# Hybrid decoder layer on one core: four merge steps built among the last branch steps, and a new order for those steps

## The chip, the cores and the metric

The kernel runs on one core of one Trainium2 chip. The metric is the device time of one execution in microseconds, as the median over several runs; lower is better.

## The reference, cut to what matters

One post-norm decoder layer over x of shape (1, 256, 1024) in float32. One input projection feeds four causal token mixers (A: RG-LRU, B: gated DeltaNet, C: stick-breaking attention, D: GLA). Each mixer's output is projected back to 1024 columns, gated, and summed; then come an output projection, a LayerNorm, and a mixture of 16 experts with top-2 routing.

```python
proj = jnp.einsum("bsd,de->bse", x, w_in)
(a_in, gdn_qkv, gdn_beta_in, gdn_decay_in, gdn_gate_in,
 sb_qkv, gla_qkv, gla_lr, gla_gate_in, merge_in) = jnp.split(proj, offsets, axis=-1)
...
gates = jax.nn.sigmoid(merge_in.reshape(b, s, N_BRANCHES, D_MODEL))
merged = jnp.zeros_like(x)
for n, y_n in enumerate((y_a, y_b, y_c, y_d)):
    merged = merged + gates[:, :, n] * jnp.einsum("bsc,cd->bsd", y_n.astype(x.dtype), w_branch[n])
return jnp.einsum("bsd,de->bse", merged, w_out)
```

## The kernel before

The program is one function, `trunk`, which emits the instructions of five engines. It has three parts: the branch steps, sixteen merge steps with the output projection behind them, and the mixture of experts.

**Precision.** A float32 product is made of three products of a faster kind: each operand is split into a high part and a remainder. For weights this is `parts` (lines 117 to 134): ScalarE casts the raw tile to `whi` (L129), VectorE subtracts to get `wlo` (L133). There are three buffers of each (NHI = 3), so a cast waits until TensorE is done with the tile three casts before it. `mm3` (L268 to L280) issues the products: sixteen on `whi` and eight on `wlo` for one 1024 x 128 block. Raw weights of 1 MB come by DMA from SyncE's queue (`fetch`, L116) into three buffers; SyncE issues in the order of the program and waits at a buffer that is not free.

**Branch steps.** The string `ORDER` lists them, and a loop calls `steps[f]` in that order. Steps with `_in` in their function's name are projections (`bi`, `gg`, `lg`, `dq`, `dv`, `cq`, `cv`, `ai`): TensorE work that depends on nothing but the weights. The others are chains with many engines in turn. Those that matter here, by the names in `ORDER`:

- `b1` (`b_s1`, L620): the second chunk of DeltaNet. TensorE `pr`, VectorE scales and adds it into `VB` (L624), TensorE `pvn` (from `VB`) and `pos`, ScalarE copies `vn` (L628), TensorE `po` (from `vn`), VectorE adds `ob` (L634), ScalarE sums the squares (`junk`, L599).
- `cw`, `ct`, `cy` (L785 to L842): stick-breaking attention in three pieces: `cw` makes scores (`pze`, `pzo`), a tanh `sth` on ScalarE (L802), two GpSimd operations and a memset (L804, L807, L809), scans on VectorE (`ss`, L811), and weights in `sth` (L813). `ct` transposes them on TensorE (`pwt`, L826) and ScalarE copies them to `wt`; `cy` multiplies by the values (`pyc`).
- `gg.1` is the second half of DeltaNet's gate projection (`ptm`, then `th` on ScalarE and `gg` on VectorE, L657 and L658); `by` norms and gates DeltaNet's output (`fb`, `ytok` L642, transposes `pyt` L646, `yth` and `ytl`); `do` and `dy` are the same for GLA; `ai.0` and `ai.1` are the RG-LRU input projection (`pcm`) with its convolution on VectorE (`xc`, L852); `al` is the RG-LRU itself: products `prg` (L862), a row of activations `tr`, `ti`, `aa` (L863 to L867), VectorE and GpSimd operations with a scan (`ya`), and a split into `yth`, `ytl`.

**Merge steps.** `merge(i)` for i = 0 to 15: projects one 256-column block of a branch's gate (48 products `pcm`), takes a tanh on ScalarE (`tg`, L897), multiplies the branch's output by its block of `w_branch` (24 products `pbr`), and adds gate times product into `acc` on VectorE (L906 to L909). The branches come in the order `MORDER = (1, 3, 2, 0)`, so steps 0 to 3 belong to B (DeltaNet), 4 to 7 to D, 8 to 11 to C, and 12 to 15 to A. From step 6 on (RS = 6) each step also issues some expert weights ahead (L946).

**What sets the order.** SyncE's queue is kept in program order. On the other four engines a scheduler decides, when the kernel is built, which ready instruction comes next, and it prefers steps that are written earlier; on the chip each engine then runs its own list in that fixed order and waits at semaphores. So the order in which steps are written decides which work stands beside a chain that waits. PSUM has eight banks: three for the projections (`mm`) and five for the rest (`pb`).

Of the kernel before, what the change touches and what calls it, by code (L numbers as in the profile page):

```python
# [29 lines left out]
NPJ = 8  # L30
NH2 = 15
RS = 6
RAW0 = 1
NHI = 3
NRA = 20
# [4 lines left out]
ORDER = """  # L40
bi.0 cc bi.1 bi.2 cq.0 bi.3 sm bi.4 cq.1 bi.5 bs gg.0 bp.0 ll bv.0 cq.2 bp.1 bo lg.0
dq.0 ba.1 lg.1 bb dq.1 dq.2 dq.3 bx.0 ba.0 dv.0 bx.1 dg bl.0.0 dv.1 bl.1.0 bl.0.1 cq.3 de
bl.2.0 da.0 bl.1.1 da.1 bv.1 cw.0 cv.0 b0 bl.2.1 rt ds cw.2 do.1 b1 ct.0 do.0 cw.1 cv.1 ct.2 cy.0
gg.1 ct.1 ai.0 cy.1 by ai.1 dy al
"""

C_A, C_GQ, C_GBD, C_GG, C_SQ, C_SV = 0, 512, 2048, 2056, 2568, 3592
# [4 lines left out]
def trunk(ctx: ExitStack, tc: tile.TileContext, a, out):  # L52
# [11 lines left out]
    rwp = [r.enter_context(tc.tile_pool(name="rw", bufs=1, side="left")) for r in rws]  # L64
    rwo = [(0, 2, 1)[(RAW0 + j) % 3] for j in range(3)]

    def turn_raw():
        rwo.append(rwo.pop(0))
# [23 lines left out]
    def Y(name, dt=F32R):  # L92
        return yp.tile([128, 4, S], dt, name=name, tag="y", bufs=NY)

    def pb(name, shape=(128, 4, 128)):
        return pbr.tile(list(shape), F32, name=name, tag="pb")
# [12 lines left out]
    def fetch(src, cuts=1):  # L109
        k, n = src.shape[1], src.shape[2]  # L110
        turn_raw()
        raw = rwp[rwo[-1]].tile([128, 2048], F32, name="raw", tag="raw")[:, :k * n]
        raw = raw.rearrange("p (k c) -> p k c", k=k)
        for c in range(cuts):
            cs = slice(c * n // cuts, (c + 1) * n // cuts)
            Q.dma_start(raw[:, :, cs], src[:, :, cs])  # L116
        return raw

    def parts(raw, k0, nk, c0, n, one=None):

        hi = wst.tile([128, 1024], F32R, name="whi", tag="whi", bufs=NHI)[:, :nk * n]
        lo = wst.tile([128, 1024], F32R, name="wlo", tag="wlo", bufs=NHI)[:, :nk * n]
        hi = hi.rearrange("p (k c) -> p k c", k=nk)
        lo = lo.rearrange("p (k c) -> p k c", k=nk)
        src = raw[:, k0:k0 + nk, c0:c0 + n]
        cuts = (slice(0, nk),) if one is None else (slice(0, nk // 2), slice(nk // 2, nk))
        for c in cuts:
            if one is None:
                A.copy(hi, src)  # L129
            else:  # L130
                A.activation(hi[:, c], src[:, c], AF.Copy, scale=one)  # L131
        for c in cuts:
            V.tensor_tensor(lo[:, c], src[:, c], hi[:, c].bitcast(F32), op=OP.subtract)  # L133
        return hi, lo
# [104 lines left out]
    for lv in range(3):  # L239
        s = 16 << lv  # L240
        m = pmask[:, lv, :]
        if s < 64:
            m = m.rearrange("p (b r) -> p b r", r=s)
# [24 lines left out]
    def mm3(o, sh, sl, mh, ml, kt, first=True, last=True, wm=False):  # L268

        for k in range(kt):  # L270
            T.matmul(o, sh(k), mh(k), start=first and k == 0, stop=False)  # L271
            if wm:
                T.matmul(o, sl(k), mh(k), start=False, stop=False)  # L273
            else:
                T.matmul(o, sh(k), ml(k), start=False, stop=False)  # L275
        for k in range(kt):
            if wm:
                T.matmul(o, sh(k), ml(k), start=False, stop=last and k == kt - 1)
            else:
                T.matmul(o, sl(k), mh(k), start=False, stop=last and k == kt - 1)  # L280

    def proj_cm(c0, raw=None, one=None):

        if raw is None:
            raw = fetch(w_in[:, :, c0:c0 + 256])
        p = pmm.tile([128, 2, S], F32, name="pcm", tag="mm")
        for b in range(2):
            hi, lo = parts(raw, 0, 8, 128 * b, 128, one)
            mm3(p[:, b, :], lambda k: hi[:, k, :], lambda k: lo[:, k, :],
                lambda k: xh[:, k, :], lambda k: xl[:, k, :], 8)  # L290
        return p
# [357 lines left out]
    def gate_in(nm, c0, ci):  # L649

        if ci == 0:
            setattr(v, nm, PJ(nm, (128, 2, 512)))
        g = getattr(v, nm)
        p = proj_tm(c0 + 256 * ci)
        for t in range(2):
            th = tmp.tile([128, 256], F32, name="th", tag="thp")
            A.activation(th, p[t], AF.Tanh, scale=0.5)  # L657
            V.scalar_tensor_tensor(g[:, t, 256 * ci:256 * ci + 256], th, 1.0, p[t], op0=OP.add, op1=OP.mult)  # L658
# [226 lines left out]
    def merge(i):  # L885

        bi, c4, c2 = i // 4, i // 2 % 2, i % 2
        b = MORDER[bi]
        if i == 0:
            v.acc = [Y("acc0", F32), Y("acc1", F32)]  # L890
        if c2 == 0:
            v.rawb = fetch(wbr[b].rearrange("(k p) c -> p k c", p=128)[:, :, c4 * 512:(c4 + 1) * 512])
        p = proj_cm(C_M + b * D + (4 * c4 + 2 * c2) * 128)
        if c2:
            turn_raw()
        tg = wst.tile([128, 2, S], F32, name="tg", tag="tg", bufs=2)
        A.activation(tg, p, AF.Tanh, scale=0.5)  # L897
        p = pb("pbr", (128, 2, S))
        hi, lo = parts(v.rawb, 0, 4, 256 * c2, 256)
        for j in range(2):  # L900
            cs = slice(j * 128, (j + 1) * 128)
            mm3(p[:, j, :], lambda k: hi[:, k, cs], lambda k: lo[:, k, cs],
                lambda k: yth[b][:, k, :], lambda k: ytl[b][:, k, :], 4)
        ac = v.acc[c4][:, 2 * c2:2 * c2 + 2, :]
        if bi == 0:
            V.scalar_tensor_tensor(ac, tg, 1.0, p, op0=OP.add, op1=OP.mult)  # L906
        else:
            V.scalar_tensor_tensor(tg, tg, 1.0, p, op0=OP.add, op1=OP.mult)
            V.tensor_tensor(ac, ac, tg, op=OP.add)  # L909
# [3 lines left out]
        bv=b_vb, b0=b_s0, b1=b_s1, by=b_y,  # L913
        gg=lambda c: gate_in("gg", C_GG, c), lg=lambda c: gate_in("lg", C_LG, c),
# [3 lines left out]
        cw=c_w, ct=c_t, cy=c_y, ai=a_in, al=a_lru, m=merge, cc=consts, ll=late_loads, rt=router_consts)  # L918
# [49 lines left out]
    def run_ahead(n):  # L968
        for _ in range(n):
            key, src = ahead.pop(0)  # L970
            W[key] = load(src, rings, NRA + NRX + NY + 4)

    for i in range(16):
        merge(i)
        if i >= RS:
            run_ahead((i + 1 - RS) * NRA // (16 - RS) - (i - RS) * NRA // (16 - RS))
        if i == 11:
            for n in range(2):
                Q.dma_start(x_sb[n], xin[:, n, :])
# [473 lines left out]
```

## Time and profile before

| | |
|---|---|
| median of 3 runs | 617.74 us (616.12 to 619.96) |
| profiled execution, its own time | 617.43 us |
| its span in the trace | 615.6 us (1.8 us lie around it) |
| branch steps | from 0 to about 221 us of the span |
| merge steps 0 to 15 | from about 212 to 353 us |
| output projection and routing | 353 to 389 us |
| experts | 389 to 604 us |
| TensorE busy | 95% of the span |

All times of rows are microseconds from the start of the span. PE is TensorE, PEld its weight load, DVE VectorE, ACT ScalarE, POOL GpSimd, SPq SyncE's DMA queue. A float32 product shows as two records on PE; a product of split parts as one. Records of PE overlap, since products are pipelined and their ends are modelled: the distance between starts tells the rate.

### The profile page before, as it was taken

The page shows a single profiled execution, that of the slowest core. Times are in us where ns is not written, and L with a number is a line of the kernel's source. Part 1 is how long each engine was busy: PE and PEld are TensorE (multiplying, and loading weights), DVE is VectorE, ACT ScalarE, POOL GpSimd, SP SyncE. Part 2 cuts the span into 40 slices and gives each one's busy share as a digit, 9 for nine tenths or more (in the row PEclk, how much of TensorE's full clock was granted, in tenths as well). Part 3 has the DMA queues.
Part 4 walks back from the last instruction along what each step waited for, and adds up shares of the span by engine and source line. Part 5 has one row for each costly group of instructions (what it writes and reads, how often), then busy time and mean ns, then how long its engine had stood idle before and what let it go on. Part 6 is the DMA issues. An engine that isn't in the chain of part 4 may idle for free. (4 is left out here: it accounts for less than half of the span.)

```text
span 615.6 us, 10554 instructions
## 1 busy us (share of the span) xinstructions
PE 587.5 (95%) x4231; PEld 459.4 (75%) x4231; DVE 323.8 (53%) x651; ACT 253.4 (41%) x413; POOL 18.8 (3%) x53
## 2 busy tenths in 40 slices
PE   6999999999988999999999999999999999999992
PEld 5999999989978999999999999633533534444351
DVE  3798887677465986555565655542210300121245
ACT  5556664563469784443434544311211211021121
POOL 3000010100111000000000000000000000000000
PEclk9999999999999999999999999999999999999996
DMA  7877453742220436588998895889999999999941
GB/s 207 230 224 196 137 162 128 210 133 71 70 70 8 156 123 201 187 301 327 357 365 300 264 404 184 304 328 399 417 414 409 414 415 409 416 417 407 417 168 71
DMA packets 86380, 160.43 MB, mean 261 GB/s; under 512 B 9963, under 2 KB 56161, under 8 KB 86326
## 3 DMA queue, kind: packets, MB, share of 16 engines
q1 hardware_dynamic: 86198, 159.44, 71.5%
q8 instruction: 35, 0.57, 0.4%
q0 software_dynamic: 128, 0.26, 0.2%
q14 instruction: 19, 0.16, 0.1%
HBM read 158.50 MB, written 1.18 MB: 259 GB/s over the span
## 5 line engine op out<-in xcount | busy, mean ns | idle before, releaser
L133 DVE TENSOR_TENSOR wlo<-raw,whi 128x1024 fp32r<-128x1024 f32 (+1 forms) x106 | 125.9, 1200 | 53.3 <-ACT whi L129 52.6
L129 ACT CAST whi<-raw 128x1024 fp32r<-128x1024 f32 x102 | 105.9, 1048 | 101.4 <-PE pcm L275 34.8
L271 PE MATMUL pcm<-xh,whi 128*128 128x256 f32 x512 | 126.1, 284 | 2.3 <-ACT whi L131 1.5
L275 PE MATMUL pcm<-xl,whi 128*128 128x256 f32 x512 | 125.0, 282 | 0.0
L271 PEld LDWEIGHTS pcm<-xh,whi 128*128 128x128 f32 x512 | 97.4, 190 | 3.2 <-ACT whi L131 1.9
L275 PEld LDWEIGHTS pcm<-xl,whi 128*128 128x128 f32 x512 | 97.4, 190 | 0.1
L280 PE MATMUL pcm<-xh,wlo 128*128 128x256 f32 x512 | 72.5, 283 | 0.3 <-DVE wlo L133 0.2
L280 PEld LDWEIGHTS pcm<-xh,wlo 128*128 128x128 f32 x512 | 65.8, 190 | 0.8 <-DVE wlo L133 0.7
L101 DVE TENSOR_TENSOR dd<-pd,dd 128x512 fp32r<-128x512 f32 (+1 forms) x18 | 11.4, 632 | 95.3 <-ACT dd L100 95.3
L1301 PE MATMUL pd<-ew,sh 128*64 128x512 f32 (+1 forms) x288 | 56.8, 546 | 0.7 <-ACT sh L1362 0.7
L1290 PE MATMUL wu<-ew,xg 128*64 128x512 f32 x256 | 57.4, 593 | 0.0
L1290 PE MATMUL wg<-ew,xg 128*64 128x512 f32 x256 | 56.7, 595 | 0.6 <-issue 0.6
L1301 PEld LDWEIGHTS pd<-ew,sh 128*64 128x64 f32 x288 | 20.4, 137 | 35.1 <-issue 30.3
L1290 PEld LDWEIGHTS wu<-ew,xg 128*64 128x64 f32 x256 | 18.5, 137 | 36.2 <-issue 34.7
L1290 PEld LDWEIGHTS wg<-ew,xg 128*64 128x64 f32 x256 | 18.1, 137 | 33.5 <-issue 32.4
L271 PE MATMUL ptm<-whi,xh 128*128 128x256 f32 x128 | 32.6, 287 | 0.0
L271 PE MATMUL pbr<-yth,whi 128*128 128x256 f32 x128 | 32.1, 284 | 0.0
L275 PE MATMUL pbr<-ytl,whi 128*128 128x256 f32 x128 | 32.0, 282 | 0.0
L273 PE MATMUL ptm<-whi,xl 128*128 128x256 f32 x128 | 31.6, 281 | 0.0
L100 ACT CAST dd<-pd 128x512 fp32r<-128x512 f32 (+1 forms) x18 | 9.7, 539 | 46.3 <-PE pd L1301 46.3
L1207 ACT ACTIVATE xg<-pxg,gbp 128x128 f32<-128x128 f32 x32 | 13.3, 456 | 36.7 <-DVE xg L1206 35.8
L1341 DVE SCALAR_TENSOR_TENSOR sh<-wu,cw,sh 128x512 f32<-128x512 f32 x8 | 6.0, 751 | 37.9 <-PE wu L1290 37.8
(421 smaller groups left out, 887.5 us busy)
## 6 DMA issues: line engine op xcount, KB each, us to landing
raw<-in_w_in_dram SPq DMA_DIRECT2D x39, 1024.0 KB, 5.3
ew<-in_w_gate_dram SPq DMA_DIRECT2D x64, 512.0 KB, 9.8
ew<-in_w_up_dram SPq DMA_DIRECT2D x64, 512.0 KB, 9.6
ew<-in_w_down_dram SPq DMA_DIRECT2D x64, 512.0 KB, 9.8
raw<-in_w_branch_dram SPq DMA_DIRECT2D x8, 1024.0 KB
raw<-in_w_out_dram SPq DMA_DIRECT2D x4, 1024.0 KB
x<-in_x_dram SPq DMA_DIRECT2D x4, 256.0 KB, 5.3
raw<-in_w_in_dram SPq DMA_DIRECT2D x2, 512.0 KB
```

The costliest lines, as they stand in the source:

```text
L100: A.copy(hi, ps)
L101: V.tensor_tensor(lo, ps, hi.bitcast(F32), op=OP.subtract)
L129: A.copy(hi, src)
L133: V.tensor_tensor(lo[:, c], src[:, c], hi[:, c].bitcast(F32), op=OP.subtract)
L271: T.matmul(o, sh(k), mh(k), start=first and k == 0, stop=False)
L273: T.matmul(o, sl(k), mh(k), start=False, stop=False)
L275: T.matmul(o, sh(k), ml(k), start=False, stop=False)
L280: T.matmul(o, sl(k), mh(k), start=False, stop=last and k == kt - 1)
L1207: A.activation(xg[1][:, 2 * kg + k, :], ps[kg][:, k, 128:256], AF.Identity, scale=g_, bias=b_)
L1290: P(T.matmul(p[r, :], xg[pr][:, k, r], W[pr, (nm, e, k // 2)][:, k % 2, :], start=k == 0, stop=k == 7))
L1301: P(T.matmul(p[r, :], hT[:, k, r], W[pr, ("wd", e, k)][:, 0, c0:c1], start=k == 0, stop=k == 3))
L1341: V.scalar_tensor_tensor(sg, pu, cw[pr // 2][:, pr % 2:pr % 2 + 1], sg, op0=OP.mult, op1=OP.mult)
```

## The change

Four merge steps (m.0 to m.3, all of branch B) are taken out of the merge loop and written into `ORDER` among the last branch steps, and these get another order: `cw.2` comes behind `b1`; `cv.1`, `cw.1`, `gg.1`, `ai.0` and `by` come forward; `ct.2`, `cy.0`, `ct.1` and `cy.1` go behind them; `al` stands between m.2 and m.3. No instruction's computation is changed, and the number of products is the same.

```diff
@@ -30,6 +30,7 @@
 NPJ = 8
 NH2 = 15
 RS = 6
+MB = 4
 RAW0 = 1
@@ -40,8 +41,8 @@
-bl.2.0 da.0 bl.1.1 da.1 bv.1 cw.0 cv.0 b0 bl.2.1 rt ds cw.2 do.1 b1 ct.0 do.0 cw.1 cv.1 ct.2 cy.0
-gg.1 ct.1 ai.0 cy.1 by ai.1 dy al
+bl.2.0 da.0 bl.1.1 da.1 bv.1 cw.0 cv.0 b0 bl.2.1 rt ds do.1 b1 cw.2 ct.0 do.0 cv.1 cw.1 gg.1
+ai.0 by ct.2 ai.1 cy.0 dy m.0 ct.1 m.1 cy.1 m.2 al m.3
 """
@@ -971,7 +972,8 @@
     for i in range(16):
-        merge(i)
+        if i >= MB:
+            merge(i)
         if i >= RS:
```

Lines below the first hunk move by one, those below the last by two. Up to the product that makes GLA's state (`pst` of `ds`) all five engines' lists are the same as before, and SyncE's and GpSimd's lists are the same throughout.

First, TensorE around `b1`, before. `VB_1984` is the operand that VectorE makes for `pvn`; the `ptm` rows are products of `gg.1`.

```order
L278 MATMUL ptm<-wlo,xh 128x256 x3
L604 MATMUL pvn<-VB_1984,XT_1629 128x128
L604 MATMUL pos<-st,gq 128x128 x4
L278 MATMUL ptm<-wlo,xh 128x256
L271 MATMUL ptm<-whi,xh 128x256
L273 MATMUL ptm<-whi,xl 128x256
L604 MATMUL pvn<-VB_1984,XT_1629 128x128
L271 MATMUL ptm<-whi,xh 128x256
L604 MATMUL pvn<-VB_1984,XT_1629 128x128
```

The same place with the change: `pol` and its second half come from `do.1`.

```order
L607 MATMUL pol<-stl,qd 128x128
L605 MATMUL pvn<-VB_1984,XT_1629 128x128 x4
L605 MATMUL pos<-st,gq 128x128 x4
L605 MATMUL po<-vn,AN_1264 128x128 x4
L800 MATMUL pze<-sk,sq 128x256
L800 MATMUL pzo<-sk,sq 128x256
```

The four `pvn` now stand together, four products of `gg.1` come before them and the other 44 behind the scores of `cw.1`, right ahead of `ai.0`.

Second, VectorE at the same place, before. `ss` is a scan of `cw.2` or `cw.1`.

```order
L811 SCALAR_TENSOR_TENSOR ss<-kp 128x256 x4
L624 SCALAR_TENSOR_TENSOR VB_1984<-pr_2194,cw__904,VB_1984 128x128
L813 SCALAR_TENSOR_TENSOR sth<-sth,ss 128x1024
L624 SCALAR_TENSOR_TENSOR VB_1984<-pr_2194,cw__904,VB_1984 128x128 x3
L634 TENSOR_TENSOR ob_2215<-po,ob_2215 128x512
```

VectorE with the change, from there to the second low part of `ai.0`:

```order
L625 SCALAR_TENSOR_TENSOR VB_1984<-pr_2173,cw__904,VB_1984 128x128 x4
L635 TENSOR_TENSOR ob_2194<-po,ob_2194 128x512
L812 SCALAR_TENSOR_TENSOR ss<-kp 128x256 x4
L665 TENSOR_TENSOR fb<-fb,ssb 128x8
L814 SCALAR_TENSOR_TENSOR sth<-sth,ss 128x1024
L812 SCALAR_TENSOR_TENSOR ss<-kp 128x256 x4
L667 RECIPROCAL fb<-fb 128x8
L814 SCALAR_TENSOR_TENSOR sth<-sth,ss 128x1024
L659 SCALAR_TENSOR_TENSOR gg<-th,ptm 128x256
L668 SCALAR_TENSOR_TENSOR fb<-fb,rqk 128x8
L643 SCALAR_TENSOR_TENSOR ytok<-ob_2100,fb,gg 128x128 x2
L134 TENSOR_TENSOR wlo<-raw,whi 128x1024
```

`VB` and `ob` of `b1` come ahead of both pairs of scans, and both pairs come ahead of the low part of `ai.0`'s second block.

Third, ScalarE at the RG-LRU, with the change: `tg` is the gate of a merge step, `whi` a cast of merge weights.

```order
L898 ACTIVATE tg<-pcm 128x512
L130 CAST whi<-raw 128x1024
L864 ACTIVATE tr<-prg,hb 128x256 x2
L867 ACTIVATE aa<-tr,ca 128x256
L864 ACTIVATE ti<-prg,hb 128x256
L864 ACTIVATE tr<-prg,hb 128x256 x2
L864 ACTIVATE ti<-prg,hb 128x256 x2
L868 ACTIVATE tr<-tr,ca 128x256
L864 ACTIVATE ti<-prg,hb 128x256
L867 ACTIVATE aa<-tr,ca 128x256 x2
L868 ACTIVATE tr<-tr,ca 128x256 x2
L867 ACTIVATE aa<-tr,ca 128x256
```

Before, all these activations stand ahead of or beside the casts of merge step 0; now they stand between the last cast of step 3 and the first cast of step 4.

## Rows read from the trace of the kernel before

**Rows 1.** The page, busy time: us, share of the span, instructions
```profile
PE 587.5 (95%) x4231; PEld 459.4 (75%) x4231; DVE 323.8 (53%) x651; ACT 253.4 (41%) x413; POOL 18.8 (3%) x53
```

**Rows 2.** Busy time by stretch: length, engines, TensorE clock, DMA share, GB/s
```profile
180.00:200.00 20.00, 16.89 (x146) 15.71 (x147) 11.22 (x25) 14.84 (x39) 1.73 (x3) 1.00 0.03 5
...
440.00:480.00 40.00, 40.00 (x192) 14.63 (x190) 4.28 (x7) 5.20 (x10) 0.00 (x0) 1.00 1.03 412
```

**Rows 3.** PE in order of time, 172 to 251: start, us, [idle before <-releaser]
```profile
173.10 1.16 PE L604 MATMUL pst<-lv,kdt 128*128 128x128 f32 x8
...
181.16 0.49 PE L604 MATMUL pvn<-VB,XT 128*128 128x128 f32 x2 [1.56 <-DVE VB L624]
...
196.91 1.06 PE L826 MATMUL pwt<-ident,sth 128*128 128x128 f32 x8 [1.95 <-DVE sth L813]
...
233.32 0.39 PE L271 MATMUL pcm<-xh,whi 128*128 128x256 f32 x1 [0.65 <-ACT whi L129]
...
250.51 0.28 PE L271 MATMUL pcm<-xh,whi 128*128 128x256 f32 x1
250.63 0.28 PE L275 MATMUL pcm<-xl,whi 128*128 128x256 f32 x1
```

**Rows 4.** PE groups of merge steps 4 to 15: count, busy us, mean ns, idle
```profile
L271 PE MATMUL pcm<-xh,whi 128*128 128x256 f32 x192 | 46.3, 280 | 0.0
```

**Rows 5.** DVE in order of time, around the two waits
```profile
175.10 1.23 DVE L133 TENSOR_TENSOR wlo<-raw,whi 128x1024 fp32r<-128x1024 f32 x1 [0.52 <-ACT whi L129]
178.42 2.44 DVE L811 TENSOR_TENSOR_SCAN ss<-kp 128x256 f32<-128x256 f32 x4 [2.09 <-POOL ss L809]
...
182.15 0.86 DVE L624 SCALAR_TENSOR_TENSOR VB<-pr,cw__904,VB 128x128 f32<-128x128 f32 x3
...
192.61 2.44 DVE L811 TENSOR_TENSOR_SCAN ss<-kp 128x256 f32<-128x256 f32 x4 [3.24 <-POOL ss L809]
```

**Rows 6.** PE in order of time, at the RG-LRU's products
```profile
215.08 0.47 PE L280 MATMUL pcm<-xh,wlo 128*128 128x256 f32 x1
215.39 1.48 PE L862 MATMUL prg<-xc,rgw 128*128 128x256 f32 x6
```

**Rows 7.** ACT in order of time, from DeltaNet's vn to its norm
```profile
183.84 0.59 ACT L628 COPY vn<-pvn 128x512 f32<-128x512 f32 x1 [4.04 <-PE pvn L604]
...
190.90 1.08 ACT L829 COPY wt<-pwt 128x512 f32<-128x512 f32 x2
...
192.60 1.09 ACT L129 CAST whi<-raw 128x1024 fp32r<-128x1024 f32 x1
193.71 1.28 ACT L665 ACT_TABLE_LOAD   x1
195.00 0.30 ACT L665 ACTIVATE fb<-fb,eps_n 128x8 f32<-128x8 f32 x1
```

**Rows 8.** POOL and DVE in order of time, 149 to 157
```profile
148.98 1.22 DVE L133 TENSOR_TENSOR wlo<-raw,whi 128x1024 fp32r<-128x1024 f32 x1
149.61 1.08 POOL L743 TENSOR_SCALAR_AFFINE_SELECT at<-at 128x512 f32<-128x512 f32 x1 [31.93 <-ACT at L742]
...
156.80 0.64 POOL L743 TENSOR_SCALAR_AFFINE_SELECT at<-at 128x512 f32<-128x512 f32 x1 [5.86 <-ACT at L742]
```

**Rows 9.** SyncE's queue: its longest wait from 335 to 440, and the last weight loads
```profile
SPq L946 <- PE pwo L273: 15.3, 2, 14.8
...
574.63 6.51 SPq L946 DMA_DIRECT2D ew<-in_w_down_dram  x8
```

**Rows 10.** Expert weights from 560 to 600: time to landing, first product of the last loads
```profile
DMA to landing us min/median/max: 7.5/8.7/9.8
...
591.40 3.67 PE L1301 MATMUL pd<-ew,sh 128*64 128x256 f32 x32 [0.73 <-ACT sh L1362]
```

**Rows 11.** The RG-LRU in order of time: first activation and last VectorE operation
```profile
214.20 0.48 ACT L863 ACTIVATE tr<-prg,hb 128x256 f32<-128x256 f32 x1
...
232.36 1.22 DVE L101 TENSOR_TENSOR ytl<-ya,yth 128x1024 fp32r<-128x1024 f32 x1 [1.11 <-ACT yth L100]
```

## The prediction, made before the changed kernel ran

> **What bounds the kernel now.** I read the page first: TensorE is busy for 95% of the span [rows 1]. That is a share over stages with different limits, so the table by stretch comes next. Between 180 and 200 TensorE is busy for only 16.89 of 20 us, at a granted clock of 1.00 (the 2.4 GHz level), while VectorE and ScalarE have 11.22 and 14.84 us of work and the DMA engines next to none (0.03) [rows 2]. Nothing is full there: it is a chain, with engines waiting in turn. The timeline of TensorE names the waits [rows 3]: 1.56 us for `VB`, 1.95 us for `sth`, 0.65 us for a `whi`. From 250.51 on, merge steps 4 to 15 run with no idle time before any product [rows 4]; products start 0.12 us apart there (250.51, 250.63), so one merge step of 72 takes about 8.5 us. The change can win at the three waits and hardly anywhere else. The last thing to read is whether the experts, at 412 GB/s with the DMA share over 1 [rows 2], would move along.
>
> **What the waits are worth.** A product's record lasts 0.28 us but the next may start 0.12 us after it, so each idle time hides 0.16 us more: 1.56 + 1.95 + 0.65 + 3 x 0.16 = 4.6 us.
>
> *The wait for VB.* VectorE starts four scans at 178.42, after 2.09 us of idleness in front of them; they last 2.44 us, and the scaled adds into `VB` stand behind them, three of the four ending at 183.0 [rows 5]. In the new order the adds follow the low part of 175.10 directly. That one ends at 176.3, four adds of 0.3 us end at 177.3. TensorE comes to `pvn` at: 174.2 (end of `pst`, whose four float32 products take 1.0 us beside the overhang [rows 3]), plus 1.0 for `pr`, 0.7 for four products of `gg.1`, 1.8 for `pol`: 177.7. The wait goes, with 0.4 us to spare. Late next is `vn`: ScalarE has the copy of `pol` and an activation of 0.3 us in front of it, ends `vn` (0.59 us [rows 7]) at 179.6, while TensorE is through `pos` at 179.3. I take 0.3 us of new wait.
>
> *The wait for sth.* In the old order the transposes of `cw.1` stand among the first products of `ai.0`, behind scans that begin at 192.61 [rows 5]. In the new order they stand behind merge step 0, some 20 us after their `sth`: the wait goes. Late next are the casts of `ai.0`, `whi` and `wlo` of its second block. ScalarE took 8.76 us from `vn` to the start of that cast (183.84 to 192.60 [rows 7]). New in that stretch: two tanh of `cw.2` and `cw.1` that stood elsewhere (1.0), three squares (0.9), two table loads and the root between them (2 x 1.28 + 0.30); gone: two copies `wt` (1.08) and one `yth` (0.5). So 12.0 us, counted from 179.0: the cast ends at 192.0. TensorE arrives at 179.6 + 1.0 (`po`) + 1.0 (scores) + 0.9 (transposes) + 1.0 (`pol`) + 1.0 (scores) + 44 x 0.12 + 24 x 0.12 = 192.7. VectorE has in front of the low part: scans from 185.2 (2.4), `sth` (1.1), scans (2.4), `sth` (1.1), a half of `gg`, `ytok` and small ones (1.1): the low part ends at about 194.5, and TensorE wants it at 194.6. The transposes `pyt` wait 0.2 us for the last `ytok`. New waits so far 0.3 + 0.2; I add 0.1 for a late start behind `pol`, 0.6 in all. Both ends: 0 if ScalarE and VectorE run one microsecond ahead of my count, 4 if each of three hand-overs is as late as the two old ones were on average (1.4 us).
>
> *The wait for whi.* Merge step 2 waited because casts stood behind the RG-LRU. With the change `al` stands behind three merge steps. Its sixteen activations stand before the first cast of step 4 in ScalarE's list: begun at about 234, with 7 us of work, they let that cast end at 242, and TensorE comes to step 4 at 245. The wait goes.
>
> **Changes of kind.** A split product put alone among float32 products takes 0.31 us to the next start instead of 0.12 [rows 6]. Before, products of `pcm` are cut by `prg` into five pieces, of which one remains, and those of `gg.1` are cut by `pvn`; four cuts fewer at 0.19 us make 0.8 us. Bounds: 0 to 1.1 us.
>
> **The shared work of GpSimd and VectorE.** In the new order GpSimd's operations of `cw.1` fall on VectorE's `sth` of `cw.2`; before, VectorE was idle during them, waiting for them (2.09 and 3.24 us [rows 5]). A mask operation of the same shape took 1.08 us on GpSimd when a VectorE subtraction ran (148.98 to 150.2), and 0.64 when none did [rows 8]. I take that difference, 0.4 us, put on the chain of `cw.1`; bounds 0 and 1.1, the length of the VectorE operation. In the Trainium skill, the page SBUF — State Buffer (Who interferes with whom) says that a VectorE instruction with two inputs in SBUF and a GpSimd instruction that reads SBUF exclude each other for a whole instruction, whoever comes first. The pair of rows agrees (the mask ends 0.5 us after the subtraction). By that rule alone the sum below would be 613.7 instead of 613.0.
>
> **A table switch.** The load takes 1.28 us, starts 0.02 us after the cast before it ends, and the root follows within 0.01 us [rows 7]; their number stays. The Trainium skill, ScalarE: Activation LUTs (What ACT_TABLE_LOAD costs), counts a drain of about 1.38 us beside each load. By that the two switches that now stand ahead of the cast would cost 2.8 us more and the sum would be about 615; the rows show no such gap, and the measurement decides.
>
> **Sum.** 4.6 + 0.8 - 0.6 - 0.4 = 4.4 us at the start of merge step 4. Behind that point the lists are the old ones, and I take the gain to pass through. Against the profiled execution's own 617.43 us (span 615.6) that is 613.0. It stands 0.3 us under the median of 617.74, so the same holds for a median.
>
> **Does it pass through the experts?** SyncE's queue waits for TensorE in the output projection, once for 14.8 us [rows 9], so the stream of expert weights starts when TensorE gets there, and comes earlier with it. If it did not, the margin counts: the last eight loads end their issue at 581.1, land 8.7 us later (589.8), and their first product starts at 591.40 [rows 9, 10].
>
> **The rivals.**
> - *All waits go, no new one.* My counts leave margins of under a microsecond, either way. For it: the ScalarE count includes squares that may run faster side by side. Against: VectorE and ScalarE are both full from 185 to 200 in the new order. Then 4.6 + 0.8 = 5.4, time 612.0.
> - *The expert stream stays where it is.* Then only the margin can be won, 591.4 - 589.8 = 1.6 us: 615.8. For it: 412 GB/s with the DMA share over 1; against: the wait of 14.8 us.
> - *It does not do what it says: waits move.* The casts of `ai.0` and `ytok` come as late as `sth` and `VB` did, some 1.4 us at three places: no gain but the cuts, 617.
> - *Slower: the RG-LRU holds up the merge.* Its chain took from 214.20 to 233.6 [rows 11], 19.4 us. In the new order it has merge casts before, in and behind it on ScalarE and VectorE, with three buffers, so one step of 8.5 us covers it. If casts of step 4 and their low parts had to wait for the whole of it, TensorE would stand 19.4 - 8.5 = 10.9 us: 613.0 + 10.9 = 623.9. It decides from the point where the first cast of step 4 ends after TensorE's arrival there; my count leaves 3 us, and of the chain only the activations stand in front.
>
> **How the numbers follow.** A measurement of this kernel can tell about 1% from no change, that is 6.2 us. My forecast has 0.56, no new wait 0.18, the stream 0.14, moved waits 0.06, slower 0.06. The whole of what I can find to win, 5.4 us, lies under 6.2; a fifth of the forecast's chance and half of the next one's lie beyond 1% by scatter or by something that I did not count: faster 0.20. Slower by over 1% is the last rival alone: 0.06. The rest, 0.74, is within 1%. The range runs from 610.6 (6.8 us won, as far as scatter carries the best case) to 617.6 (moved waits), and leaves out the slower rival and the far ends of the others.
>
> **What would show it.** Right: no wait of `pvn` for `VB`, none of `pwt` for `sth`, merge step 4 starting at about 246 instead of 250.51, steps of 8.5 us without idle time behind it, and the experts' last products at about 587. Wrong: TensorE waiting for `whi` or `wlo` of `ai.0` by more than a microsecond, `pyt` for `ytok`, a first cast of step 4 that ends after 246, or step 4 early and the end unmoved.

## The result, and the profile after

The changed kernel takes 612.70 us (median of six runs, 611.42 to 614.47), the kernel before 617.24 beside it; the ratio of the runs on record is 0.9916, 95% interval 0.9892 to 0.9939 (the quotient of these two medians alone is 0.9926, 4.5 us). That is within 1%, and the median is 0.3 us from the forecast of 613.0. The profiled execution took 614.47, with a span of 612.7 against 615.6.

The waits of TensorE, from the end of `pst` to the first product of merge step 4 (174.80 to 247.63; columns: us in total, times, longest):

```profile
PE pcm L281 <- DVE wlo L134: 1.1, 1, 1.1
```

The three waits of [rows 3] are gone and one is new. In order of time on TensorE:

```profile
173.80 1.16 PE L605 MATMUL pst<-lv,kdt 128*128 128x128 f32 x8
...
177.98 1.06 PE L605 MATMUL pvn<-VB,XT 128*128 128x128 f32 x8
...
196.15 1.22 PE L281 MATMUL pcm<-xh,wlo 128*128 128x256 f32 x8 [1.13 <-DVE wlo L134]
197.21 1.18 PE L647 MATMUL pyt<-ident,ytok 128*128 128x128 f32 x8
198.22 1.04 PE L827 MATMUL pwt<-ident,sth 128*128 128x128 f32 x8
...
247.63 0.28 PE L272 MATMUL pcm<-xh,whi 128*128 128x256 f32 x1
```

`pvn` stands in one piece without idle time, where it came in pieces behind 1.56 us. The transposes `pwt` have no wait either. But the low part of `ai.0` is late: 1.13 us of idle time, 1.29 us more to the next start than the usual 0.12. Merge step 4 begins 2.88 us earlier than in [rows 3].

The same stretches as in [rows 2], and the groups of merge steps 4 to 15 that answer to [rows 4]:

```profile
180.00:200.00 20.00, 18.87 (x156) 17.54 (x156) 14.48 (x27) 18.09 (x46) 4.82 (x6) 1.00 0.15 43
440.00:480.00 40.00, 40.00 (x192) 14.64 (x190) 4.28 (x7) 4.61 (x8) 0.00 (x0) 1.00 1.03 412
```
```profile
L272 PE MATMUL pcm<-xh,whi 128*128 128x256 f32 x192 | 46.3, 280 | 0.0
```

TensorE is busy for 18.87 of the 20 us instead of 16.89, VectorE and ScalarE for 3.3 us more each: more of the work fits into the same 20 us. The experts run at the same 412 GB/s. The page shows how little such a change moves a share (95% before), and that GpSimd, with the same 53 instructions, is busy for 20.2 us instead of 18.8:

```profile
PE 586.7 (96%) x4231; PEld 458.9 (75%) x4231; DVE 323.9 (53%) x651; ACT 253.1 (41%) x413; POOL 20.2 (3%) x53
```

Those 1.4 us lie on the chain that ends in the new wait. GpSimd, then VectorE, in order of time:

```profile
183.44 0.63 POOL L805 TENSOR_SCALAR_AFFINE_SELECT sth<-sth 128x512 f32<-128x512 f32 x1 [19.39 <-ACT sth L803]
184.16 1.04 POOL L808 TENSOR_SCALAR kp<-sth 128x1024 f32<-128x1024 f32 x1
...
187.03 1.08 POOL L805 TENSOR_SCALAR_AFFINE_SELECT sth<-sth 128x512 f32<-128x512 f32 x1 [1.78 <-ACT sth L803]
188.19 1.97 POOL L808 TENSOR_SCALAR kp<-sth 128x1024 f32<-128x1024 f32 x1
```
```profile
187.59 0.53 DVE L665 TENSOR_TENSOR fb<-fb,ssb 128x8 f32<-128x8 f32 x1
188.05 1.21 DVE L814 SCALAR_TENSOR_TENSOR sth<-sth,ss 128x1024 f32<-128x1024 f32 x1
190.20 2.44 DVE L812 TENSOR_TENSOR_SCAN ss<-kp 128x256 f32<-128x256 f32 x4 [0.94 <-POOL ss L810]
...
192.67 1.23 DVE L814 SCALAR_TENSOR_TENSOR sth<-sth,ss 128x1024 f32<-128x1024 f32 x1
...
194.87 1.22 DVE L134 TENSOR_TENSOR wlo<-raw,whi 128x1024 fp32r<-128x1024 f32 x1
```

The pair of GpSimd operations for `cw.2` takes 0.63 and 1.04 us; the same pair for `cw.1` takes 1.08 and 1.97, 1.38 us more, while VectorE ends a scan and runs `fb` and `sth`. `kp` ends 0.9 us behind `sth` of `cw.2` (189.26), and its twin of `cw.2` takes 1.04 in all: by these rows it did next to nothing beside `sth`. Read on from there: VectorE stands idle for 0.94 us for it, then scans, `sth`, and at last `wlo`.

Downstream the gain passes whole, as [rows 9, 10] let expect. SyncE still waits 14.8 us for the output projection, which begins 2.88 us earlier, and the last expert products come at 588.44 instead of 591.40:

```profile
SPq L947 <- PE pwo L274: 14.8, 1, 14.8
```
```profile
588.44 3.67 PE L1303 MATMUL pd<-ew,sh 128*64 128x256 f32 x32 [0.73 <-ACT sh L1364]
```

One difference has nothing to do with the change. TensorE and VectorE at 114, far ahead of it:

```profile
114.83 0.66 PE L548 MATMUL px<-ident,XX 128*128 128x128 f32 x4 [0.80 <-DVE XX L543]
```
```profile
114.08 0.69 DVE L543 TENSOR_TENSOR XX<-x,m 128x512 f32<-128x512 f32 x1 [4.63 <-DMA x<-s]
```

In the profile of before, VectorE waited 2.40 us there for the same small transfer, and TensorE not at all. So the end of `pst` lies 0.61 us later in this profile (174.80 against 174.19), and I compare the *stretch* from there to merge step 4: 76.3 us before, 72.8 after, 3.5 us.

### The profile page after: what moved, and what is told of

The parts are those of the page before. It is cut to its first block, busy times and chain, and to the rows that moved or that the text cites. A ratio compares the mean times of both kernels' runs of the same rounds, so it can differ in the third digit from the quotient of the medians.

```text
span 612.7 us, 10555 instructions
## 1 busy us (share of the span) xinstructions
PE 586.7 (96%) x4231; PEld 458.9 (75%) x4231; DVE 323.9 (53%) x651; ACT 253.1 (41%) x413; POOL 20.2 (3%) x53
```

## The experiments

All stretches in one table. A wait is the start-to-start distance of two products less 0.12 us.

| run | end of pst | step 4 | stretch | waits in it | ratio to before (95%) |
|---|---|---|---|---|---|
| before | 174.19 | 250.51 | 76.3 | VB 1.71, sth 2.11, whi 0.82 | |
| after | 174.80 | 247.63 | 72.8 | wlo 1.29 | 0.9916 (0.9892 to 0.9939) |
| e1 | 173.52 | 246.35 | 72.8 | wlo 1.65 | 0.9918 (0.9895 to 0.9941) |
| e2 | 174.40 | 248.29 | 73.9 | wlo 0.74, sth 1.17, ytok 0.62 | 0.9949 (0.9930 to 0.9968) |
| e3 | 174.07 | 248.50 | 74.4 | ytok 2.02, 0.44, 0.53 | 0.9958 (0.9944 to 0.9972) |
| e4 | 174.05 | 248.16 | 74.1 | wlo 0.64, ytok 0.47, wlo 1.49 | 0.9949 (0.9930 to 0.9968) |
| e5 | 174.23 | 249.22 | 75.0 | wlo 1.28, pyc 1.02, whi 1.04 | 0.9957 (0.9939 to 0.9976) |
| e6 | 174.97 | 250.65 | 75.7 | VB 1.72, sth 2.11 | 0.9978 (0.9959 to 0.9997) |
| e7 | 174.54 | 251.19 | 76.7 | sth 2.95, whi 0.58 | 0.9970 (0.9949 to 0.9990) |
| e8 | 173.59 | 248.39 | 74.8 | wlo 1.28, xc 1.83 | 0.9953 (0.9935 to 0.9970) |
| e9 (before) | 174.04 | 250.35 | 76.3 | VB 1.71, sth 2.26, whi 0.81 | |
| e10 (before) | 174.08 | 251.92 | 77.8 | VB 1.71, sth 2.11, whi 0.81 | |
| e11 | 173.19 | 247.03 | 73.8 | wlo 0.74, ytok 1.83 | 0.9948 (0.9928 to 0.9968) |

**e1, the changed kernel again.**

> The changed kernel once more. Measure: the stretch from the end of the products of pst (d_st) to the first product of merge step 4, 76.3 us in the profile of before and 72.8 in that of after. Theory S (the 0.8 us that TensorE waited for px on VectorE's XX at 114, well ahead of the change, is the landing time of a small transfer, which differs from run to run): the stretch is 72.8 +- 0.2 again, GpSimd's kp of cw.1 takes 1.97 +- 0.1 again, and the wait for XX is another number, anywhere from 0 to 1.5 us. Rival (that wait belongs to the changed kernel): 0.8 us again. Ratio to the kernel before: 0.993 if 3.5 us of the stretch is all there is, 0.990 or less if the first measurement (0.9916) hides more.

The stretch is 72.8 and `kp` takes 1.97 us again; `px` starts at 113.46 and does not wait. Theory S holds: the wait at 114 is a transfer's. The ratio says 0.992 again, which is 5 us (4.4 by the medians, 617.22 and 612.83) and not 3.5; e9 and e10 take that up.

**e2, `sth` of `cw.2` kept off GpSimd.** The line leaves the function of `cw` for a new one, `c_m`; the other pieces call it at the old place, `cw.2` only at the start of `ct.2`. The edit, cut to this line:

```diff
-        V.scalar_tensor_tensor(th, th, 1.0, ss[:, :, 1:kl + 1], op0=OP.add, op1=OP.mult)
+        one = 1.0
+        if gi == 2:
+            one = act.tile([128, 1], F32, name="one2")
+            V.tensor_scalar(one, v.ss[1][:, 3, 0:1], 0.0, 1.0, op0=OP.mult, op1=OP.add)
+        V.scalar_tensor_tensor(th, th, one, v.ss[gi], op0=OP.add, op1=OP.mult)
```

> VectorE's sth of cw.2 is made to wait for the scans of cw.1 (its scalar 1.0 is read from a tile that is computed from the last scan), so that it no longer runs beside GpSimd's kp of cw.1. Theory P (the 1.3 us that TensorE waits for wlo in ai.0 are GpSimd's kp and mask, drawn out by VectorE's sth and fb): kp takes 1.05 us instead of 1.97, the scans of cw.1 begin 0.9 us earlier behind the mask, the wait for wlo falls from 1.3 to 0.3 or less. As sth now stands behind ytok, the transposes of ct.2 wait for it by 0.5 to 1.2 us, so that the stretch is 72.3 to 73.0 (ratio to before 0.991 to 0.995). Rival D (VectorE's list is full there, whatever GpSimd does): kp stays at about 2 us, the wait for wlo at 1.3, and the later sth comes on top: 73.5 to 74.5.

GpSimd, then VectorE:

```profile
186.64 1.08 POOL L805 TENSOR_SCALAR_AFFINE_SELECT sth<-sth 128x512 f32<-128x512 f32 x1 [1.78 <-ACT sth L803]
187.81 1.05 POOL L808 TENSOR_SCALAR kp<-sth 128x1024 f32<-128x1024 f32 x1
```
```profile
187.21 0.53 DVE L665 TENSOR_TENSOR fb<-fb,ssb 128x8 f32<-128x8 f32 x1
188.89 2.44 DVE L812 TENSOR_TENSOR_SCAN ss<-kp 128x256 f32<-128x256 f32 x4 [1.15 <-POOL ss L810]
...
193.56 1.22 DVE L134 TENSOR_TENSOR wlo<-raw,whi 128x1024 fp32r<-128x1024 f32 x1
```

`kp` takes 1.05 us; the mask, still beside the end of a scan and `fb`, 1.08. Counted from the end of `pst`, `wlo` begins at 19.16 us instead of 20.07 in after and 20.08 in e1, 0.91 us earlier, just what `kp` lost. The list of VectorE is not what made the difference: the scans begin 0.91 us earlier too, behind an idle wait for GpSimd, and from there to `wlo` it is 4.67 us in both. So VectorE's `sth` causes that part of the wait, and theory D falls on `kp`, though the stretch lies in its range. The wait is 0.74 us and not the 0.3 that P had, since TensorE comes there 0.36 us earlier than in after; against e1, where it comes as early, the wait falls by just those 0.91. The time isn't won: `sth`, put behind `ytok`, is now late for `pwt` (1.17), and `ytok` for `pyt` (0.62). Theory P had the first of these and not the second, and its stretch is 0.9 short.

**e3, `cw.1` behind `gg.1`.**

```diff
-do.1 b1 cw.2 ct.0 do.0 cv.1 cw.1 gg.1
+do.1 b1 cw.2 ct.0 do.0 cv.1 gg.1 cw.1
```

> cw.1 stands behind gg.1 instead of ahead of it; GpSimd's operations of cw.1 then begin some 4 us later, behind sth of cw.2, and in VectorE's list the wlo of ai.0 stands ahead of the scans of cw.1. Theory P (the chain over GpSimd holds up wlo): no wait for wlo, the stretch is 71.5 plus some 0.5 for transposes of ytok that stand singly among split products: 71.5 to 72.6, ratio to before 0.988 to 0.992. Rival D (ScalarE and VectorE full from 185 to 200): the wait moves to another tile of ai.0 or ai.1 (whi, wlo, ytok) and the stretch stays at 72.8 or more.

No wait for `wlo`, as P says, yet the stretch is 74.4: the second set of `ytok` comes late by 2.02, 0.44 and 0.53 us. Rival D was right on the sum. It named the place only in part: the wait went to `ytok` of `dy`.

**e4, `by` behind `ai.1`.**

```diff
-ai.0 by ct.2 ai.1 cy.0
+ai.0 ct.2 ai.1 by cy.0
```

> by (the norm of DeltaNet) stands behind ai.1 instead of behind ai.0, so two ytok operations (0.62 us) no longer stand ahead of wlo on VectorE; the chain of cw.1 over GpSimd is unchanged. Theory P: kp is drawn out as before (1.9 to 2.0 us), the wait for wlo falls by those 0.6 us to 0.7, and the stretch is 72.2 (ratio 0.991). Rival (another input, the cast whi, sets the start of wlo): the wait stays at 1.3, the stretch at 72.8; if ytok then comes late for its transposes, 73 to 74.

The wait for `wlo` falls by 0.65 us to 0.64, with `kp` at 1.97: VectorE's list sets its start, as P says. Then `ytok` (0.47) and a `wlo` of merge step 0 (1.49) are late: 74.1, where P had 72.2 and the rival at most 74.

**e5, the new branch order alone, and e6, the merge steps alone.** e5 has MB = 0 and the list ending in `ai.0 by ct.2 ai.1 cy.0 dy ct.1 cy.1 al`; e6 the old list ending in `ai.1 dy m.0 m.1 m.2 al m.3`.

> The new order of the branch steps with all sixteen merge steps behind them, as in the kernel before. The stretch from the end of pst to the first product of merge step 4 is 76.3 us before, 72.8 after. Theory P (what pays is that cw.2, cw.1 and ct.1 stand elsewhere): the waits for VB (1.7) and sth (2.1) go, the wait for wlo in ai.0 (1.3 to 1.7) comes, a wait for whi behind the RG-LRU (0.8) stays: 73.8 to 74.2, ratio 0.9945 to 0.997. Rival M (what pays is that merge steps lie between branch steps): without them the transposes, copies and the RG-LRU wait in turn, 75.5 or more.

> The old order of the branch steps, with merge steps 0 to 2 ahead of al and step 3 behind it. Theory P: only the wait for whi behind the RG-LRU (0.8) goes, those for VB (1.7) and sth (2.1) stay; the stretch is 75.2 to 75.6, ratio 0.998. Rival M: most of the 3.5 us, 74 or less.

TensorE's waits in e5:

```profile
195.58 1.21 PE L281 MATMUL pcm<-xh,wlo 128*128 128x256 f32 x8 [1.12 <-DVE wlo L134]
209.07 1.99 PE L840 MATMUL pyc<-wt,sv 128*64 128x128 f32 x32 [0.86 <-DVE ytl L105]
232.04 0.38 PE L272 MATMUL pcm<-xh,whi 128*128 128x256 f32 x1 [0.87 <-ACT whi L130]
```

e5 wins 1.3 us: the waits for `VB` and `sth` go, that for `wlo` comes, as P says, but `pyc` of `cy.1` waits as well (0.86, idle), which P had not, so that the stretch of 75.0 lies between the ranges of P and M. e6 wins 0.6, the wait for `whi`. Alone they come to 2.0 us, together to 3.5: the merge steps cover the wait at `pyc` that the new branch order makes, and the one at `whi` that it leaves. P and M each hold half of the truth.

**e7, `cw.2` alone.**

> Of the change only that cw.2 stands behind b1; the rest of the order and the merge as before. Theory P: the wait for VB goes (1.7), but the transposes of ct.2, left among the products of gg.1, come to their sth 2.9 us too early (TensorE there at about 186.4, sth of cw.2 ends at 189.3), and by that delay those of ct.1 wait for nothing: 76.3 - 1.7 - 2.1 + 2.9 = 75.4, and up to 76.2 with a wait for whi as before. Rival (each move counts by itself): VB's 1.7 us and no more, 74.6, with pwt of ct.1 waiting 2 us.

`VB` no longer waits, and `pwt` of `ct.2` waits 2.95 us where 2.9 was expected: a step that makes a tile and the one that reads it have to move together. But the stretch is 76.7 instead of 75.4 (76.0 with the 0.58 for `whi`). The table by stretch shows why (the last three columns are TensorE's granted clock, DMA share and GB/s):

```profile
186.00:188.00 2.00, 0.36 (x4) 0.16 (x2) 2.00 (x5) 1.98 (x6) 1.14 (x2) 1.00 0.00 0
188.00:190.00 2.00, 0.85 (x6) 0.88 (x7) 1.06 (x2) 0.91 (x5) 1.96 (x2) 0.87 0.00 0
190.00:192.00 2.00, 2.00 (x16) 1.67 (x16) 2.00 (x4) 1.42 (x4) 0.00 (x0) 0.50 0.03 8
192.00:194.00 2.00, 2.00 (x19) 1.67 (x16) 2.00 (x4) 1.24 (x2) 0.00 (x0) 0.78 0.00 0
```

Behind the long wait the granted clock is at 0.50, the 1.2 GHz level, for about 3 us: eight transposes take 1.57 us from start to start instead of 0.8 to 1.0. Without its waits the stretch has 73.1 us of work here, 71.7 in before; I put these 1.4 us down to the spell.

**e8, the RG-LRU ahead of merge step 0.**

> The changed kernel with the RG-LRU (al) ahead of merge step 0 instead of behind step 2. Theory P (a step of 8.5 us behind each cast covers what stands in front of it): sixteen activations (7 us) stand among the first casts of the merge, so that TensorE waits for a whi of steps 0 to 2 by 0.6 to 3 us: stretch 73.4 to 75.8. Rival of the prediction (the merge waits for the whole RG-LRU): some 10.9 us, 83.7. No wait at all: 72.8.

74.8, in the range, by another wait than P named: not `whi`, but the first RG-LRU products for `xc` (1.83), which VectorE ends late. The sixteen activations hold up no merge step, and the 10.9 us of the slower rival do not come even with `al` first.

**e9 and e10, the kernel before again.**

> The kernel before, unchanged, for another profile. Its runs come at several mean granted clocks (0.992, 0.989, 0.986 and 0.984), those of the changed kernel mostly at 0.992 and 0.989, and the profile shown of before is one at 0.989 (one spell of about 3 us at the 1.2 GHz level near 384). Theory C (the waits of the old order bring one more such spell, and the change takes it away with them): in a profile at 0.986 TensorE falls to 0.50 for some 3 us just behind the wait for sth or VB, at 180 to 200, and the stretch is 1.5 us longer than 76.3, about 77.8. Rival (the second spell lies outside the changed stretch, such as that at 124 in the runs of merge_only and cw2_only): the stretch is 76.3 again. A profile at 0.989 or 0.992 decides nothing.

> The same once more: at a mean clock of 0.986, theory C expects a spell at 0.50 between 180 and 200 and a stretch of about 77.8; its rival a spell elsewhere and 76.3.

One each. e9 (mean clock 0.986) has its second spell at 124, and the stretch is 76.3:

```profile
124.00:126.00 2.00, 2.00 (x10) 1.88 (x10) 0.92 (x2) 1.95 (x4) 0.00 (x0) 0.53 0.78 267
126.00:128.00 2.00, 2.00 (x13) 2.00 (x12) 0.17 (x1) 1.99 (x2) 0.00 (x0) 0.62 0.00 0
```

e10 (0.987) has it behind the wait for `sth`, and the stretch is 77.8, as theory C has it:

```profile
194.00:196.00 2.00, 0.84 (x8) 0.64 (x6) 2.00 (x4) 1.97 (x3) 0.00 (x0) 1.00 0.00 0
196.00:198.00 2.00, 1.20 (x11) 1.24 (x12) 2.00 (x3) 1.41 (x4) 0.00 (x0) 0.96 0.00 0
198.00:200.00 2.00, 2.00 (x11) 2.00 (x11) 1.96 (x10) 2.00 (x4) 0.00 (x0) 0.50 0.32 72
200.00:202.00 2.00, 2.00 (x14) 2.00 (x14) 2.00 (x6) 1.97 (x3) 0.00 (x0) 0.69 1.04 351
```

So in one execution of before a spell of 1.5 us stands behind the wait for `sth`; in the other two profiles of before, and in e6, none does. The runs taken together show how much the spells weigh. By mean granted clock of the run: at 0.991 and more, five runs of before have a mean of 615.4 us and six of after one of 612.0; at 0.988 to 0.990 it is 616.9 (17 runs) and 613.7 (5 runs). At like clock the change is worth 3.2 to 3.5 us, the stretch's 3.5. But 39 of 61 runs of before lie at 0.987 or less, and only one of twelve of after. Over all of them the means are 617.6 and 612.8, 4.8 us apart: 3.5 from the waits and some 1.3 from fewer spells. That these spells go with the waits, as theory C has it, is not shown, and e6 speaks against it: there the waits for `VB` and `sth` stand at their full length, and yet only one of ten runs lies at 0.987 or less, against 21 of the 30 runs of before beside it. The mean of e6 is 1.7 us under theirs (616.06 against 617.77), while its stretch is 0.6 us shorter. The profiles of e6 and e7 also have a spell at 124, ahead of all that was edited. Why the changed kernel has fewer spells stays open.

**e11, e2 with `ct.2` behind `ai.1`.**

```diff
-ai.0 by ct.2 ai.1 cy.0
+ai.0 by ai.1 ct.2 cy.0
```

> As e2 (sth of cw.2 waits for the scans of cw.1, so that it doesn't run beside GpSimd's kp), with ct.2 behind ai.1 as well, so that its transposes need sth some 6 us later. Theory P: kp 1.05 us, the wait for wlo 0.4 to 0.8 as in e2 (0.74), none for sth of cw.2: a stretch of 71.8 to 72.4, against 72.8, ratio to before 0.989 to 0.992. Rival (every move here makes another tile late, as in e2 to e4): ytok, fl or a wlo of the next step comes late by a microsecond, 72.8 or more.

No wait for `sth` any more, 0.74 for `wlo` as in e2, and then 1.83 for `ytok`, behind the product at 204.25: 73.8. The rival holds. No version here beats the changed kernel.

## Why the prediction was right, and where it was not

- *The waits for VB, sth and whi.* Right, all three: 4.6 us gone, with no wait in front of `pvn`, `pwt` or step 4.
- *New waits, 0.6 us.* The 0.3 for `vn` did not come. The transposes `pyt` take 1.0 us instead of 0.85, the 0.2 that I put there. The low part of `ai.0` I had at 194.5 against TensorE at 194.6; TensorE came at 194.86 and it ended at 196.09.
- *The shared work of GpSimd and VectorE, 0.4 us.* This is the step that was mis-sized: 1.38 us, more than my upper bound of 1.1. I had priced one operation by the pair in [rows 8], but the mask and `kp` stand in a row and both meet VectorE, and `kp` meets a 1.21 us operation from its start. e2 shows 0.92 of the 1.38 directly (`kp` 1.05 instead of 1.97); that the 0.45 of the mask comes from the scan and `fb` beside it is read from the trace and was not tried. The rule of the Trainium skill's page SBUF — State Buffer (Who interferes with whom), that such a pair excludes each other for a whole instruction, gave an estimate of 1.1 us, which was the nearer price for this term. The rows agree with it: `kp` has nearly its whole length (0.90 us) behind the end of `sth`.
- *Changes of kind, 0.8 us.* Too much. Without its waits the stretch is 71.7 us before and 71.5 and 71.2 in after and e1: 0.1 to 0.5 us. What the missing cuts of `pcm` give, 0.3 to 0.5 us summed from start to start, the RG-LRU's products take back: sixteen of them last 2.69 us from start to start in before, cut in among others, and 3.21 in after, where fourteen stand together.
- *Table switches.* As the rows had it. ScalarE in after, two switches with 0.02 us between a load and what stands before and behind it:

```profile
187.26 1.28 ACT L666 ACT_TABLE_LOAD   x1
188.56 0.30 ACT L666 ACTIVATE fb<-fb,eps_n 128x8 f32<-128x8 f32 x1
188.76 0.29 ACT L600 ACTIVATE junk<-ol 128x128 f32<-128x128 f32 x1
188.96 0.19 ACT L600 ACTIVATION_READ_ACCUMULATOR junk<-ol 128x1 f32 x1
189.17 1.28 ACT L658 ACT_TABLE_LOAD   x1
190.46 0.39 ACT L658 ACTIVATE th<-ptm 128x256 f32<-128x256 f32 x1
```

  The cast that I had ending at 192.0 begins at 191.04 and ends at 192.08. The drain beside each load that the Trainium skill counts, on the page ScalarE: Activation LUTs (What ACT_TABLE_LOAD costs), has no room in these rows.
- *The sum.* 4.4 us forecast for the stretch, 3.5 measured: 4.6 of waits and some 0.2 of cuts, less 1.3. In the profile 0.6 of it is lost ahead of the change, at `px`, and that execution took 614.47. That the median is only 0.3 us from 613.0 is luck. Two errors go opposite ways: 0.9 us too much for the stretch, and about 1.3 us of fewer spells at the lower clock, a term that I had not in the sum at all and whose cause stays open.
- *Through the experts.* Right: 2.88 us at the output projection, 2.96 at the last products. The rival of a fixed stream falls.
- *The signs.* The missing waits for `VB` and `sth` and merge steps of 8.5 us without idle time came as said; step 4 and the last products came 1.6 and 1.4 us later than said. One sign of being wrong came too: TensorE waited for `wlo` of `ai.0` by more than a microsecond (1.29).
- *Rivals.* No new wait: wrong by the 1.29. Moved waits: wrong for the change itself, and what e2, e3, e4, e5 and e11 did. The slower one: e8 shows no wait of a merge step for the RG-LRU.

## What to carry to other kernels

Where two engines hold each other up, as GpSimd and VectorE do here, price every operation of the chain by itself, and by the whole length of the other engine's instruction; then look whose chain the sum stands on. A reordering that removes waits is worth what it removes less what is late next, and the producer, the reader and the work that covers them have to move together: here the parts alone gave 1.3 and 0.6 us, together 3.5. Before comparing two profiles of a small change, subtract what differs in front of it.

## What the runs showed of the hardware that I had not expected

- TensorE's granted clock falls to 0.50 for about 3 us in some executions of a program and not in others: behind the 2.11 us wait for `sth` in e10 but not in before, behind 2.95 us in e7, at 124 in e9 but not in before (TensorE is busy in each of the ten microseconds ahead of it). Between two programs it also differs in the router's products `spread`, which neither edits: 5.46 us in e1 and 3.84 in e2 for the same 32 products. Where I could measure it, a spell costs 1.4 to 1.6 us. TensorE in e1, then in e2:

```profile
379.03 5.46 PE L1143 MATMUL spread<-lnr,ident 128*128 128x128 f32 x32 [0.32 <-DVE lgt L1033]
```
```profile
380.95 3.84 PE L1155 MATMUL spread<-lnr,ident 128*128 128x128 f32 x32 [0.33 <-DVE lgt L1045]
```

- A VectorE operation on 128x8 numbers, `fb` at 187.59, took 0.53 us; in before, where GpSimd is idle, the same one takes 0.17. By these rows both engines lose, and a tiny instruction too: the mask beside it went from 0.63 to 1.08.
- The same small transfer (`x`, 64 KB), issued at 108.04 and 107.71, landed after 4.1 us in the profile of before and after 6.3 in that of after, so that VectorE waited 2.40 and 4.63 us; TensorE's distance between the two programs goes by it from 0.34 us ahead to 0.6 behind.
